# Raw memory rows and a factor behind the products in the opening of a two-layer encoder trunk

## The chip, the cores and the metric

The kernel runs on one core of one Trainium2 chip. The metric is the device time of one execution in microseconds; a kernel's time is the median of its runs. Engines are named as the profile names them: PE (TensorE, the matrix products), PEld (its weight loads), DVE (VectorE), ACT (ScalarE), POOL (GpSimd) and SP (SyncE, which here only issues transfers). L12 is line 12 of the kernel before, unless the text says otherwise.

## The reference

Two layers, each with a token mixer (dilated windows in the first, grouped queries with a rotary table in the second), cross-attention into 256 memory tokens, a gate and an output projection. D_MODEL is 1024, the sequence has 512 tokens. What matters here is the way from the memory rows to the keys and values of the first layer:

```python
def rmsnorm(x, g):
    xf = x.astype(jnp.float32)
    y = xf * lax.rsqrt(jnp.mean(xf * xf, axis=-1, keepdims=True) + EPS)
    return (y * g.astype(jnp.float32)).astype(x.dtype)
...
def memory_attention(q_mem, mem_h, w_kv, qn_g, kn_g):
    ...
    kv = jnp.einsum('bnd,de->bne', mem_h, w_kv).reshape(Bn, N, 2, MEM_HEADS, HEAD_DIM)
    k = rmsnorm(kv[:, :, 0], kn_g)
    v = kv[:, :, 1]
...
    for i in range(DEPTH):
        h = rmsnorm(x, norm_g[i])
        mem_h = rmsnorm(mem, mem_norm_g[i])
```

`mem_h` is `mem` times a factor for each row (the reciprocal root mean square) times the norm's row `mem_norm_g[i]`. The factor of a row is one number for a whole token, so it may stand in front of the product with `w_kv` or behind it. `x` is normalized in the same way by `norm_g[i]`.

## The kernel before

All arithmetic is on the chip. Products have nearly full float32 precision: each operand is split into an upper part (rounded to the product's format) and a lower part (what is left), and each product runs as three, upper by upper, lower by upper, upper by lower. In `proj_t`, `mm_early` issues the first two (L173, L174) for each of four blocks of the inner dimension, and `mm_late` then the third (L177). The large projections use a Strassen-like scheme of seven products (`s_chunk`), whose operands are sums of quarters of x and of the weights.

**Order.** Each engine works through its own instructions in the order in which the program issues them, and so do the queues of transfers; waits between engines follow from the data. The order is written by hand. A driver counts slots: after each group of products `W.advance()` and `drv.tick()` issue what is due (weight casts, norms, splits). Work that is spawned with a delay appears in the tick of that slot; what follows a finished group (`drv.release`, `drv.free`) one or two groups later.

**Weights** come as pieces of 128x1024 float32 (512 KB), issued on SP's queue by `W.dma` as long as fewer than a set number are live. `W.hi` casts a piece on ACT into the upper part `wh` (L309), `W.lo` makes the lower part `wo` on DVE (L319); both live in rings of four tiles, so the fifth cast waits for the last product with the first piece. For the Strassen chunk, `W.sum` also adds pieces on DVE (L278) or by accumulating transfers from POOL's queue.

**The opening** (L938 to L1046). SP's queue: the two norm rows as single rows of 4 KB, the two blocks of memory rows (128 tokens each) with weights between them, more weights, the four blocks of x and weights. `row_bank` (L622) spreads a norm row over 128 partitions by a product with a column of ones; this is done for both rows, two halves each, eight passes at L627. The memory rows go through `norm_1` (squares with a sum on ACT or DVE, then three small operations on POOL for the factor), `norm_2` (L497: row block times factor times norm row, on DVE), `turn4` (four transpositions on PE, L503) and `split` (L159: upper part on ACT, lower part on DVE). `ahead` is called by `chunk` ahead of a group and issues the other three half blocks: one ahead of the second group, two ahead of the third. It also copies x's norm row out of the PSUM banks (L1024).

**Keys and values.** `mem_kv` (L657) runs two projections over two blocks and two halves of the inner dimension: four groups for the keys, four for the values. The keys' evacuation `ev_k` takes head-wise squares on ACT (`head_sq`, L594), a factor on POOL (`rstd_of`, L450 and L451), multiplies on DVE (`head_mul`, L599), transposes and splits. `ev_v` writes half the values as an upper part on ACT (L676) and a lower one on DVE (L679).

**x.** `prep` (L963) starts at slot 2: `norm_1` of a block in each slot, `norm_2` one slot later, `first_t` (transpositions and splits of the top half, L161, L164) one slot after that, then differences for the Strassen scheme. `rm` keeps the memory rows' factors for the second layer.

## Time and profile before

| what | value |
|---|---|
| median of 3 runs | 956.26 us (955.84 to 957.37) |
| the profiled execution's own time | 955.53 us |
| its span in the profile | 953.7 us |
| PE busy | 942.1 us, 99% of the span |
| DVE busy | 789.9 us, 83% |
| ACT busy | 680.5 us, 71% |
| POOL busy | 332.9 us, 35% |
| moved by transfers | 202.98 MB |

In rows of the timeline the first number is the start and the second the duration, both in microseconds from the start of the span; then engine, line, operation, the tiles written and read with their shapes, how many such instructions the row merges, and in brackets how long the engine was idle before the row and what ended that. In rows of the chain of waits there are start, duration and what the time went to. In groups, the numbers behind the bar are the busy time in microseconds and the mean duration in nanoseconds, then the idle time before them. A row of transfers gives the number, the size of each and the median time in microseconds from its issue to its landing. "Issue" as a cause means that the profile shows nothing that the engine waited for.

### The profile page before, as it was taken

The numbers are of one execution on the slowest core, as the hardware profiler recorded it, in microseconds if no ns is written. First come the engines' busy times: TensorE is split into PE (matmuls) and PEld (weight loads), VectorE is DVE, ScalarE is ACT, GpSimd is POOL, SyncE is SP. The second block draws the span as 40 slices with busy tenths as digits, with TensorE's granted clock in tenths as the row PEclk, the third lists the DMA queues.
The fourth block names the chain that finished last, engine by engine and source line by source line (L and its number), as shares of the span: only waits on it lengthen the run. The fifth ranks groups of instructions, "written<-read, shape, count | busy, mean of one in ns | idle before, by whom it ended". The sixth has DMA issues, their size and how long they took to land.

```text
span 953.7 us, 16568 instructions
## 1 busy us (share of the span) xinstructions
PE 942.1 (99%) x5682; PEld 831.7 (87%) x5682; DVE 789.9 (83%) x1410; ACT 680.5 (71%) x1701; POOL 332.9 (35%) x478
## 2 busy tenths in 40 slices
PE   8999999999999999999999999999899999999998
PEld 4879888888888888888889998888899999998886
DVE  4898776878888888979788899977988898769982
ACT  5875689686868686867775667547778877879860
POOL 1512423557454546463726111213232330111110
PEclk9999999999999999999999999999999999999999
DMA  9989946969687869696877989979966697877524
GB/s 357 329 205 344 301 113 175 295 117 267 145 262 155 264 156 265 155 263 135 236 185 184 260 199 252 291 264 299 246 153 133 193 237 173 210 208 179 126 56 128
DMA packets 85913, 202.98 MB, mean 213 GB/s; under 512 B 25027, under 2 KB 34499, under 8 KB 85829
## 3 DMA queue, kind: packets, MB, share of 16 engines
q1 hardware_dynamic: 66676, 138.94, 42.7%
q0 software_dynamic: 17856, 60.83, 34.4%
q10 hardware_dynamic: 1296, 2.16, 0.6%
q8 instruction: 45, 0.74, 0.3%
q14 instruction: 40, 0.32, 0.1%
HBM read 155.96 MB, written 11.34 MB: 175 GB/s over the span
## 4 chain that ended last, share of the span: by engine, by line
PE 90%; DVE 5%; ACT 2%; DMA 1%; issue 1%; POOL 0%; DVEq 0%; SPq 0%; ACTq 0%; POOLq 0%
PE pj L174 23%; PE pj L173 23%; PE pj L177 23%; PE qT L606 2%; DVE wo L319 2%; PE sa L1162 1%; PE oo L1270 1%; PE pt L1249 1%; PE ptb L1472 1%; PE sa L1158 1%; PE ob L177 1%; PE xT L503 1%; PE row L627 1%; PE pmt L736 1%; PE ob L174 1%
## 5 line engine op out<-in xcount | busy, mean ns | idle before, releaser
L319 DVE TENSOR_TENSOR wo<-wl,wh 128x1024 fp32r<-128x1024 f32 x255 | 316.0, 1245 | 6.2 <-ACT wh L309 6.0
L309 ACT CAST wh<-wl 128x1024 fp32r<-128x1024 f32 x255 | 268.3, 1059 | 30.5 <-PE pj L174 14.4
L173 PE MATMUL pj<-wh,hS 128*128 128x512 f32 (+1 forms) x448 | 157.4, 365 | 0.8 <-DVE sn L403 0.8
L174 PE MATMUL pj<-wh,hS 128*128 128x512 f32 (+1 forms) x448 | 152.2, 353 | 0.6 <-DVE hS L570 0.6
L173 PE MATMUL pj<-wh,h 128*128 128x512 f32 (+1 forms) x336 | 117.9, 364 | 0.0
L174 PE MATMUL pj<-wh,h 128*128 128x512 f32 (+1 forms) x336 | 114.2, 353 | 1.1 <-DVE h L570 1.1
L451 POOL TENSOR_TENSOR rstd<-mse,half 128x4 f32<-128x4 f32 (+2 forms) x96 | 100.9, 1051 | 8.0
L177 PE MATMUL pj<-wo,hS 128*128 128x512 f32 (+1 forms) x448 | 100.0, 352 | 0.2 <-DVE wo L319 0.2
L173 PEld LDWEIGHTS pj<-wh,hS 128*128 128x128 f32 x448 | 84.8, 189 | 11.3 <-DVE sn L403 1.0
L174 PEld LDWEIGHTS pj<-wh,hS 128*128 128x128 f32 x448 | 84.9, 190 | 11.0 <-DVE hS L570 0.8
L450 POOL TENSOR_SCALAR mse<-hss 128x4 f32<-128x4 f32 (+1 forms) x86 | 42.5, 494 | 126.3 <-ACT junk L594 122.1
L177 PEld LDWEIGHTS pj<-wo,hS 128*128 128x128 f32 x448 | 74.6, 189 | 12.4 <-DVE wo L319 0.6
L594 ACT ACTIVATE junk<-sn 128x128 f32<-128x128 f32 x264 | 79.1, 309 | 1.0 <-DVE sn L397 1.0
L386 ACT COPY sn<-pj 128x512 f32<-128x512 f32 x116 | 64.5, 590 | 21.1 <-PE pj L177 20.3
L1106 POOL TENSOR_TENSOR ta<-sn,tabs 128x128 f32<-128x128 f32 (+1 forms) x64 | 35.5, 562 | 119.0 <-DVE sn L599 92.2
L177 PE MATMUL pj<-wo,h 128*128 128x512 f32 (+1 forms) x336 | 74.8, 352 | 0.0
L174 PEld LDWEIGHTS pj<-wh,h 128*128 128x128 f32 x336 | 63.7, 190 | 8.8 <-DVE h L570 1.3
L173 PEld LDWEIGHTS pj<-wh,h 128*128 128x128 f32 x336 | 63.6, 189 | 7.3
L403 DVE TENSOR_TENSOR sn<-pj,sn 128x512 f32<-128x512 f32 x87 | 59.3, 683 | 10.1 <-PE pj L177 7.7
L293 POOL DMA_DIRECT2D wl<-wl x33 | 29.2, 884 | 106.8 <-DVE wo L319 59.6
L177 PEld LDWEIGHTS pj<-wo,h 128*128 128x128 f32 x336 | 56.0, 189 | 8.8
L283 POOL DMA_DIRECT2D wl<-wl x33 | 31.3, 982 | 62.5 <-DVE wl L278 18.5
(246 smaller groups left out, 2358.7 us busy)
## 6 DMA issues: line engine op xcount, KB each, us to landing
wl<-in_wall_dram SPq DMA_DIRECT2D x222, 512.0 KB, 7.3
wl<-wl POOLq DMA_DIRECT2D x66, 512.0 KB, 5.6
wl<-in_wall_dram POOLq DMA_DIRECT2D x42, 512.0 KB, 8.3
od<-o SPq DMA_DIRECT2D x11, 256.0 KB, 5.6
og<-od SPq DMA_DIRECT2D x10, 256.0 KB, 7.6
m<-in_mem_dram SPq DMA_DIRECT2D x4, 512.0 KB, 5.7
x<-in_x_dram SPq DMA_DIRECT2D x4, 512.0 KB, 8.9
v0d<-sn SPq DMA_DIRECT2D x8, 256.0 KB, 7.3
```

The costliest lines, as they stand in the source:

```text
L173: T.matmul(o, a, b, start=start, stop=False, skip_group_check=True)
L174: T.matmul(o, c, d, start=False, stop=False, skip_group_check=True)
L177: T.matmul(o, a, b, start=False, stop=stop, skip_group_check=True)
L283: G.dma_start(self.tile[key], self.tile[c, "T1", x], accum_op=ALU.add)
L309: A.copy(wh, self.tile[self.items[i]])
L319: V.tensor_tensor(wo, self.tile[key], wh.bitcast(F32), ALU.subtract)
L386: A.copy(t, b)
L403: V.tensor_tensor(t, b, t, ALU.subtract if q == "12" else ALU.add)
L450: G.tensor_scalar(e, ss, EPS, None, ALU.add)
L451: G.tensor_tensor(r, e, half[:, 0:n], ALU.pow)
L594: A.activation(jk, p[:, j * 128:(j + 1) * 128], AF.Square, scale=QS, accum_out=ss[:, j:j + 1])
L1106: G.tensor_tensor(ta[:, 0:n], xn[:, 0:n, 0:32], ropeA[:, 0, b, s0:s0 + n], ALU.mult)
```

## The change

The memory rows of the first layer are no longer multiplied by their factor ahead of the transposition: they are multiplied by the norm's row alone, split and projected, and the factor of each row comes into the evacuation: as the scale of the keys' head-wise squares and a multiply on POOL of the keys' head factors (`ev_k`), and as the scale of the values (`ev_v`). `rm` grows from two columns to six: the factor, the factor by QS, half the factor.

The norm's row of the memory comes in two ways: its first half is spread by one product with the column of ones (two passes), its second half and the whole row for x come as transfers that write all 128 partitions. The memory rows are loaded as four half blocks. The first half of the norm's row is issued on ACT's queue, the rest on SP's in a new order. The products of x's row, its copies and the `busy` product are gone. Four products on a tile of zeros (`idle`) are issued: two ahead of the spread row, one behind it, one behind the first transposition.

The transpositions and splits of the three later half blocks are issued in the middle of a group, between the early and the late products (`mid` instead of `pre`): one in the first group, two in the second, so each a group earlier than before. The first half block's upper part is written by DVE instead of ACT. All squares of the memory rows are on ACT. The casts of the third and fourth weight piece are issued in the first group.

```diff
 TCKW = {}
 NBIG, NM4, NS2, SCRATCH = 7, 23, 14, 2048
 RING, LEAD = 4, 2
-BULK, ACTIVE, SET_AT, WARM, MEM_B, PREP_Y, PREP_B, HALF, SET_B = 2, 2, 15, 1, 14, 1, 1, {"a": 3, "b": 3, "o": 0}, 9
+BULK, ACTIVE, SET_AT, IDLE, MEM_B, PREP_Y, PREP_B, HALF, SET_B = 2, 2, 15, (2, 1, 1), 14, 1, 1, {"a": 3, "b": 3, "o": 0}, 9
 MEM_STEP = 1, 1
 MEM_D = 4
 DIRECT, DIRECT_B = (7,), (4, 5, 6, 7)
...
 
     W = Weights()
 
-    def chunk(units, nb, group, evac, pre=None):
+    def chunk(units, nb, group, evac):
 
         ps = [None] * nb
         for u in range(units):
...
             for b in range(nb):
                 if u == 0:
                     ps[b] = pj()
-                if pre:
-                    pre(u, b)
                 group(w, u, b, ps[b])
                 drv.free()
                 if u == units - 1:
...
     mask = tabs[:, 0:512]
     ropeA = tabs[:, 512:2048].rearrange("p (c b s e) -> p c b s e", c=2, b=4, s=6)
     half = pool.tile([128, 8], F32, name="half")
-    rm = pool.tile([128, 2], F32, name="rm")
+    rm = pool.tile([128, 6], F32, name="rm")
     ones = tabs[0:1, 0:128]
     V.memset(half, -0.5)
     V.memset(ones, 1.0)
...
 
     NAT = [nat(b) for b in range(4)]
 
-    def proj_t(act, sels, evac, pre=None):
+    def proj_t(act, sels, evac, mid=None):
 
         def group(w, u, b, p):
             for k in range(4):
                 kk = 4 * u + k
                 mm_early(p, sels[b](act, 0, kk), w[k][0], sels[b](act, 1, kk), w[k][0], kk == 0)
+            if mid:
+                mid(u, b)
             for k in range(4):
                 kk = 4 * u + k
                 mm_late(p, sels[b](act, 0, kk), w[k][1], kk == 7)
-        chunk(2, len(sels), group, evac, pre)
+        chunk(2, len(sels), group, evac)
 
     part = {}
 
...
         put("22", f22)
         yield 1
 
-    def head_sq(p, n=4):
+    def head_sq(p, n=4, by=QS):
         ss = sm(n, "hss")
         for j in range(n):
             jk = small.tile([128, 128], F32, tag="junk", name="junk", bufs=2)
-            A.activation(jk, p[:, j * 128:(j + 1) * 128], AF.Square, scale=QS, accum_out=ss[:, j:j + 1])
+            A.activation(jk, p[:, j * 128:(j + 1) * 128], AF.Square, scale=by, accum_out=ss[:, j:j + 1])
         return rstd_of(ss, n)
 
     def head_mul(p, r, n=4, dst=None):
...
         t = m4(name="row")
         nc.sync.dma_start(t, src.to_broadcast([128, D]))
         rows[name] = halves(t)
-
-    def row_bank(name, times=1, bank=at):
-
-        r = [bank("row") for _ in range(2)]
-        for j in (1, 0):
-            for _ in range(times):
-                T.matmul(r[j], ones, rows[name][j][0:1, :], start=True, stop=True)
-        return r
 
     Ms = {}
 
...
         drv.soon(lambda: V.scalar_tensor_tensor(lo, q, gain, hi.bitcast(F32), ALU.mult, ALU.subtract))
         yield 1
 
-    def mem_kv(layer, M, pre=None):
+    def mem_kv(layer, M, mid=None):
         kt_ = [m4(F32R, "kmT").rearrange("p (h t) -> p h t", h=4) for _ in range(2)]
         vt_ = [m4(F32R, "vm").rearrange("p (b e) -> p b e", b=2) for _ in range(2)]
 
         def ev_k(b, p):
-            r = head_sq(p)
+            r = head_sq(p) if layer else head_sq(p, by=rm[:, 2 + b:3 + b])
 
             def rest():
+                if not layer:
+                    G.tensor_scalar(r, r, rm[:, b:b + 1], None, ALU.mult)
                 xn = head_mul(p, r)
                 yield 2
                 q = transpose4(xn)
...
 
         def ev_v(b, p):
 
-            A.activation(vt_[0][:, b], p, AF.Copy, scale=0.5)
+            h = 0.5 if layer else rm[:, 4 + b:5 + b]
+            A.activation(vt_[0][:, b], p, AF.Copy, scale=h)
             if b and LO_V[layer]:
                 yield LO_V[layer]
-            V.scalar_tensor_tensor(vt_[1][:, b], p, 0.5, vt_[0][:, b].bitcast(F32), ALU.mult, ALU.subtract)
-            yield 1
-
-        proj_t(M, NAT[:2], ev_k, pre)
+            V.scalar_tensor_tensor(vt_[1][:, b], p, h, vt_[0][:, b].bitcast(F32), ALU.mult, ALU.subtract)
+            yield 1
+
+        proj_t(M, NAT[:2], ev_k, mid)
         proj_t(M, NAT[:2], ev_v)
         return kt_, vt_
 
...
     xt = [m4(name="x") for _ in range(4)]
     rows = {}
     mt = [m4(name="m") for _ in range(2)]
+    row0 = m4(name="row0")[0:1, 0:512]
+    nc.scalar.dma_start(row0, mem_norm_g[0:1, 0:512])
     nc.scalar.dma_start(ident, ident_d)
-    row0 = m4(name="row0")[0:1, :]
-    nc.sync.dma_start(row0, mem_norm_g[0:1, :])
-    rows["m0"] = halves(row0)
-    row1 = m4(name="row1")[0:1, :]
-    nc.sync.dma_start(row1, norm_g[0:1, :])
-    rows["x0"] = halves(row1)
+    row1 = s2(name="row1")
+    nc.sync.dma_start(mt[0][:, 0:512], mem[0:128, 0:512])
+    W.dma(2)
+    nc.sync.dma_start(mt[1][:, 0:512], mem[128:256, 0:512])
+    nc.sync.dma_start(row1, mem_norm_g[0:1, 512:1024].to_broadcast([128, 512]))
     for b in range(2):
-        nc.sync.dma_start(mt[b], mem[b * 128:(b + 1) * 128])
-        W.dma(1)
+        nc.sync.dma_start(mt[b][:, 512:1024], mem[b * 128:(b + 1) * 128, 512:1024])
+    W.dma(2)
+    row_load("x", norm_g[0:1, :])
     W.dma(2)
     tabA = s2(name="tabA")[:, 0:256].rearrange("p (b c d) -> p b c d", b=2, c=4)
     grA = s2(name="grA")[:, 0:192].rearrange("p (s c) -> p s c", s=6)
     nc.sync.dma_start(gc, gcol)
     for c in range(4):
         nc.sync.dma_start(xt[c], xv[c])
-        if c % 2:
+        if c % 2 and c < 3:
             W.dma(2)
     H, H2 = {}, {}
     xb = [halves(t) for t in xt]
...
                             grA[:, None].to_broadcast([128, 4, 6, 32]), ALU.mult)
             yield 1
 
-    first = row_bank("m0", WARM)
-    gain = row_bank("x0", 1, pj)
-    rows["x"] = halves(m4(name="row"))
-
-    def busy(n):
-
-        T.matmul(at("busy")[:, 0:n], ones, rows["m0"][0][0:1, 0:n], start=True, stop=True)
-
+    z = s2(F32R, "z")
+    V.memset(z.bitcast(F32), 0.0)
+
+    def idle(n):
+
+        for _ in range(n):
+            T.matmul(at("idle"), z[:, 0:128], z, start=True, stop=True)
+
+    idle(IDLE[0])
+    row = at("row")
+    T.matmul(row, ones, row0, start=True, stop=True)
     mb, M = [halves(t) for t in mt], Act(NM)
-    nst = [norm_1(mb[0], True)]
+    ss = [sm(2, "ss") for _ in range(2)]
+    mg = {}
+
+    def times(b, j):
+
+        t = mg[b, j] = s2(name="mg")
+        V.tensor_tensor(t, mb[b][j], row1 if j else row, ALU.mult)
+
+    def square(b, j):
+
+        A.activation(s2(name="sq"), mb[b][j], AF.Square, scale=1.0 / 32.0, accum_out=ss[b][:, j:j + 1])
+
+    def factor(b):
+
+        e = sm(1, "mse")
+        G.tensor_tensor(e, ss[b][:, 0:1], ss[b][:, 1:2], ALU.add)
+        r = rstd_of(e, 1)
+        for k, by in enumerate((1.0, QS, 0.5)):
+            G.tensor_scalar(rm[:, 2 * k + b:2 * k + b + 1], r, by, None, ALU.mult)
+
+    def place_m(b, j, act=True, p=None):
+
+        cs = slice(b * 128, (b + 1) * 128)
+        split(M.block(0, j, cs), M.block(1, j, cs), p or turn4(mg[b, j], None, None), act)
+
+    square(0, 0)
+    times(0, 0)
+    idle(IDLE[1])
+    p = turn4(mg[0, 0], None, None)
+    idle(IDLE[2])
     W.hi(True)
-    norm_2(mb[0], nst[0], first, (0,))
-
-    def mid():
-        busy(128)
-        W.lo()
-        nst.append(norm_1(mb[1]))
-
-    turn4(mb[0][0], M.block(0, 0, slice(0, 128)), M.block(1, 0, slice(0, 128)), mid)
+    place_m(0, 0, False, p)
     W.hi(True)
-    norm_2(mb[1], nst[1], first, (0,))
     W.lo()
+    times(1, 0)
+    W.lo()
+    for b, j in ((1, 0), (0, 1), (1, 1)):
+        square(b, j)
+    for b in range(2):
+        times(b, 1)
+        factor(b)
 
     def ahead(u, b):
 
+        if (u, b) == (0, 0):
+            place_m(1, 0)
+            W.hi(True)
+            W.hi(True)
         if (u, b) == (0, 1):
-            for j in range(2):
-                A.copy(rows["x"][j], gain[j])
-            norm_3(mb[1], M, 128, 0)
-            for c in range(2):
-                G.tensor_copy(rm[:, c:c + 1], nst[c])
-            for c in range(2):
-                norm_2(mb[c], nst[c], first, (1,))
-        if (u, b) == (1, 0):
-            for c in range(2):
-                norm_3(mb[c], M, 128 * c, 1)
+            place_m(0, 1)
+            place_m(1, 1)
 
     drv.spawn(prep(), PD)
     drv.spawn(setup(), SET_AT)
```

## The prediction

> **What bounds the kernel now.** I read the page first, then the stretches, the opening in order of time, and last the chain of waits.
>
> ```profile
> span 953.7 us, 16568 instructions
> PE 942.1 (99%) x5682; PEld 831.7 (87%) x5682; DVE 789.9 (83%) x1410; ACT 680.5 (71%) x1701; POOL 332.9 (35%) x478
> ```
>
> TensorE lacks 953.7 - 942.1 = 11.6 us of the whole span. A microsecond that the opening gives or takes therefore has almost nowhere to be absorbed once TensorE alone sets the pace. Between 30 and 60 us it does not: VectorE is as full as TensorE there.
>
> ```profile
> 30.00:40.00 10.00, 10.00 (x56) 8.54 (x55) 9.81 (x13) 7.59 (x22) 6.48 (x10) 1.00 0.93 331
> 40.00:50.00 10.00, 10.00 (x52) 8.32 (x51) 9.53 (x13) 6.13 (x10) 2.37 (x4) 1.00 0.99 243
> 50.00:60.00 10.00, 9.79 (x43) 7.54 (x42) 9.84 (x15) 8.34 (x13) 2.01 (x3) 1.00 0.92 170
> 59.38 1.19 PE L177 MATMUL pj<-wo,hS 128*128 128x512 f32 x4 [0.21 <-DVE wo L319]
> ```
>
> The columns are the stretch, PE, PEld, VectorE, ScalarE and POOL busy, granted clock, transfer share and GB/s. VectorE is busy 9.81, 9.53 and 9.84 of 10, the transfers are at 0.92 to 0.99, and the one wait of TensorE, at 59.38, is for VectorE. So the opening has two clocks that both must move: TensorE, and VectorE's unbroken queue from 30 us on. Now the first 12 us:
>
> ```profile
> 1.40 0.36 SPq L950 DMA_DIRECT2D m<-in_mem_dram  x1
> 2.35 7.16 PE L627 MATMUL row<-row,tabs 1*128 1x512 f32 x8 [2.35 <-DMA row<-in_mem_norm_g_dram]
> 5.26 0.63 ACT L490 ACTIVATE sq<-m 128x512 f32<-128x512 f32 x1 [3.04 <-DMA m<-in_mem_dram]
> 6.66 1.04 ACT L309 CAST wh<-wl 128x1024 fp32r<-128x1024 f32 x1 [0.68 <-DMA wl<-in_wall_dram]
> 7.32 0.75 DVE L497 SCALAR_TENSOR_TENSOR m<-m,rstd,row 128x512 f32<-128x512 f32 x1 [1.36 <-POOL rstd L451]
> 9.45 1.12 PE L503 MATMUL xT<-ident,m 128*128 128x128 f32 x4
> 10.60 0.58 ACT L161 CAST act<-xT 128x512 fp32r<-128x512 f32 x1 [1.30 <-PE xT L503]
> 11.22 0.69 DVE L164 TENSOR_TENSOR act<-xT,act 128x512 fp32r<-128x512 f32 x1 [2.01 <-ACT act L161]
> 11.24 0.79 PE L173 MATMUL pj<-wh,act 128*128 128x512 f32 x1
> 13.61 0.43 PE pj L173
> 15.20 0.93 PE pj L177 x4
> 18.47 0.23 PE pj L173
> ```
>
> The normalized memory half is ready at 7.32 + 0.75 = 8.1 us, but TensorE is inside the eight row passes until 9.5 us; only then come the transpositions, the split, and the first product at 11.24. The last three rows are steps of the chain: a product costs 0.43 until about 15.2 (the group of four there takes 0.93, 0.23 each) and 0.23 after. What follows the first group:
>
> ```profile
> 9.37 0.19 POOL L492 TENSOR_TENSOR mse<-ss 128x1 f32<-128x1 f32 x1 [2.08 <-ACT sq L490]
> 17.97 0.50 PE L174 MATMUL pj<-wh,act 128*128 128x512 f32 x1 [0.22 <-DVE act L164]
> 18.98 0.63 ACT L490 ACTIVATE sq<-x 128x512 f32<-128x512 f32 x1
> 19.15 2.35 DVE L319 TENSOR_TENSOR wo<-wl,wh 128x1024 fp32r<-128x1024 f32 x2
> 20.40 1.15 POOL L492 TENSOR_TENSOR mse<-ss 128x1 f32<-128x1 f32 x1 [9.60 <-ACT sq L490]
> 23.06 1.40 DVE L497 SCALAR_TENSOR_TENSOR x<-x,rstd,row 128x512 f32<-128x512 f32 x2
> 28.34 0.65 ACT L490 ACTIVATE sq<-x 128x512 f32<-128x512 f32 x1
> 29.57 1.08 ACT L161 CAST h<-xT 128x512 fp32r<-128x512 f32 x2
> 30.19 1.29 DVE L164 TENSOR_TENSOR h<-xT,h 128x512 fp32r<-128x512 f32 x2 [1.00 <-ACT h L161]
> 30.66 0.57 POOL L451 TENSOR_TENSOR rstd<-mse,half 128x1 f32<-128x1 f32 x1
> 31.40 0.68 DVE L599 TENSOR_TENSOR xn<-pj,rstd 128x512 f32<-128x512 f32 x1
> 34.26 1.22 DVE L278 TENSOR_TENSOR wl<-wl 128x1024 f32<-128x1024 f32 x1
> 37.26 0.57 POOL L451 TENSOR_TENSOR rstd<-mse,half 128x1 f32<-128x1 f32 x1
> 37.92 0.68 DVE L599 TENSOR_TENSOR xn<-pj,rstd 128x512 f32<-128x512 f32 x1
> ```
>
> VectorE's last idle microsecond ends at 30.19, and what ends it is ScalarE's split of x's first block (29.57), itself queued behind the squares at 28.34. That is where the shift must be measured.
>
> **First product.** Six of the eight row passes go; so do the squares, POOL's factor and the multiply by it ahead of the first transposition. The new path: a zero fill on VectorE (no row for one of 128x512; between nothing and the 0.69 of L164, taken near the top, since the half it fills is as long), two fill products at 0.43, and the row pair at 7.16 / 4 = 1.8. From 1.0 that is 1.0 + 0.7 + 0.9 + 1.8 = 4.4 us, or 3.7 with a free fill. The first half block, now first on its queue and half as large, lands near 0.73 + 3.86 - 0.65 = 3.9 (0.73 is where the first issue stands now; 3.86 is the landing at 5.26 less the issue at 1.40; 0.65 is half of 1.3 per 512 KB, from the 1.4 between the landings that ended the waits before 5.26 and 6.66 and the 1.25 of the rows under transfers below). Multiply 0.7, transposition 1.1, split on VectorE instead of ScalarE 0.6 to 0.7: first product at 6.9, against 11.24, **4.3 earlier**. The first weight lands near 5.2 and its cast of 1.04 ends at 6.3, in time. The third fill product ends before the multiply does, the fourth before the split: nothing, covered by these; each would cost 0.43 without the cover.
>
> **Second group.** Seven more products at 0.43 after the lower half (7.6) end at 10.6. The next rows' transposition (0.5 to 1.1), cast 0.58 and split 0.69 put the group's second product at 12.6 to 13.0, against 17.97: 5 earlier. VectorE alone comes to the same: from 6.2 it has the two passes of the first split, three multiplies and the next split, 6 x 0.69, and two weight residues at 2.35 / 2, 6.5 together, so 12.7. It holds this point there even if TensorE were faster. The group then ends at 13 + 7 x 0.23 + 8 transpositions (0.9) + 0.93 = 16.2.
>
> **ScalarE from there.** One group of the page is needed:
>
> ```profile
> L594 ACT ACTIVATE junk<-sn 128x128 f32<-128x128 f32 x264 | 79.1, 309 | 1.0 <-DVE sn L397 1.0
> ```
>
> With four weight tiles split early, the casts of the fifth and sixth move one group ahead. They wait for the ring slots that this group's end frees (a new wait; queued behind it are the squares of x's first two blocks): 16.2 + 2 x 1.0 = 18.2. Squares of x0 and x1, 1.25 each (the 29.57 - 28.34 of x2's): 20.7; four head squares, 79.1 / 264 = 0.3 each: 21.9; two casts: 23.9; squares of x2: 25.2. Then comes the split that started at 29.57: **4.4 earlier**. x0's normalization comes 23.06 - 18.98 = 4.1 after its squares start, so at 22.3 to 23.7, and its transposition ends at 24.6, in time; TensorE waits some 1.5 us ahead of it and is then about 4.4 earlier too.
>
> **Transfers.** The new rows are 256 KB and 512 KB spread over all partitions.
>
> ```profile
> 599.75 0.43 SPq L260 DMA_DIRECT2D wl<-in_wall_dram  x1
> 601.10 0.33 SPq L619 DMA_DIRECT2D row<-in_mem_norm_g_dram  x1
> wl<-in_wall_dram SPq DMA_DIRECT2D x1, 512.0 KB, 7.2
> row<-in_mem_norm_g_dram SPq DMA_DIRECT2D x1, 512.0 KB, 7.1
> ```
>
> A spread row of this size landed 601.10 + 7.1 = 608.2, 1.25 after the weight ahead of it (599.75 + 7.2): it costs what any 512 KB cost, 1.3. So the queue grows by 1.5 x 1.3 = 1.9 us. By the new order ten such pieces (six weights, one and a half of memory rows, one and a half of the new rows, and x0 itself) land after the first half block, so x0 near 3.9 + 13 = 16.9, x1 18.2, and x2 after two more weights 22.1; squares want them at 18.2, 19.5 and 23.9. The fifth and sixth weights, just ahead of x0, land at 14.3 and 15.6 and are wanted at 16.2. Margin 1.3 at the least, so nothing. The next narrow place is the sum at 34.26, wanted at 30 to 31 now:
>
> ```profile
> 18.33 0.33 SPq L260 DMA_DIRECT2D wl<-in_wall_dram  x1
> wl<-in_wall_dram SPq DMA_DIRECT2D x1, 512.0 KB, 10.2
> ```
>
> The piece it needs landed at 28.5 and will at 30.4: just in time, 0 to 0.5.
>
> **The factor behind the products.** Keys get a second POOL multiply of 128x4 ahead of VectorE's `head_mul`, queued behind the next x block's norm.
>
> ```profile
> L450 POOL TENSOR_SCALAR mse<-hss 128x4 f32<-128x4 f32 x2 | 2.0, 1001 | 2.1 <-ACT junk L594 2.0
> ```
>
> That norm ended at 30.66 + 0.57 = 31.2 and at 37.8, against heads at 31.40 and 37.92. With 1.0 (the row above; the operation itself has no row) the heads wait until 32.2 and 38.8, 0.8 and 0.9. The second is mostly covered: after the first, VectorE is 0.8 late and POOL, which waits for ScalarE, is not. I take **0.9** for both; ends 0.3 and 1.8. POOL's six extra factor operations of the opening end near 13, wanted at 20.8: nothing. Scales that become columns: taken at 0.1, between nothing and 0.2.
>
> The Trainium skill (SBUF — State Buffer, Who interferes with whom) says that a VectorE instruction with two SBUF inputs and a GpSimd instruction that reads SBUF exclude each other for a whole instruction. The rows agree: the same 128x1 add took 0.19 at 9.37 and 1.15 at 20.40 beside the residue. By this rule POOL runs freely once VectorE stands waiting for it, which would make the stall 0.3 to 0.5 rather than 0.9.
>
> **Sum.** 4.4 - 0.9 - 0.1 - 0.1 (half of what the sum may wait, rounded down) = 3.3 us at 30 us, on VectorE; TensorE has more, so at 59.38 VectorE decides, and 3.3 travels to the end. The profiled execution took 955.53, so 952.2; the median of the runs, 956.26, lies 0.73 above it. **Predicted: 956.26 - 3.3 = 953.0.** Its own range: with a late clock (1.3, third rival), a stall of 1.8, 0.5 at the sum and 0.2 for the scales 0.6 of the 4.4 is left, but not all of them are likely at once; I take a gain of 1.9 to 4.7, so 951.6 to 954.4.
>
> The Trainium skill (TensorE: Matmul & The Clock Gate, Part 1) has the clock double after about 3.4 us of sustained activity. Here TensorE was inside row passes from 2.35 to 9.5 and the step stayed 0.43 until 15.2, 3.9 after the first full product: one-row passes did not count as activity. If the zero products count, the rate is up before the first group; since VectorE holds the second group to about 12.7, that is worth 0.4 at most.
>
> **Rivals.**
> - *Transfers bind the stretch to 60 us (slower).* For: share 0.92 to 0.99, and everything from the sum at 34.26 on needs pieces queued behind the new rows. If that piece and its followers set VectorE's pace, the start is worth nothing and 786 KB are added: 1.9 us at the opening's pace, 3.2 at the 243 GB/s of 40 to 50 us, so 958.2 to 959.5 on the median. It decides once the piece of 28.5 lands 5.8 late or the pieces behind it have no slack. Against: that 5.8 of slack (34.26 - 28.5), and that in the view of waits of the first 60 us no engine but ScalarE at 6.66 and the first memory rows waits for a transfer. 0.16.
> - *POOL binds.* Each added multiply costs VectorE its full turn twice, up to 1.9 each: 4.4 - 3.8 - 0.1 = 0.5, 955.8. For: POOL's norm ends 0.1 to 0.2 before the heads. Against: VectorE's first wait covers the second. 0.16.
> - *The slow rate lasts a window longer.* If it takes 7.8 instead of 3.9 after the first product, some nine products and four transpositions cost 0.2 or 0.15 more, of which 0.6 is hidden by VectorE: 1.3 to 1.9 lost, 954.6. For: gaps between the first products are more than before. 0.12.
> - *No stall at all and full rate early:* 4.4 + 0.4 or more, below 951.6. 0.08.
>
> **Chances.** Forecast 0.48. Faster by over 0.2% (1.9 us, about what a measurement can tell from none): forecast, last rival and half of the third, 0.62. Within: the second and the rest of the third, 0.22. Slower: 0.16. The range reaches from half of the last rival, 950.9, to the lower edge of the first, 958.2, leaving about 0.18 out.
>
> **What would show it.** First product near 6.9; `row` two passes; second product of group two near 12.8. The split of x's first block near 25.2 and VectorE unbroken from 25.8, with one idle below 1 us ahead of the first `xn` ended by POOL. Squares of x not ended by a transfer. A wait of the sum at L278 for a transfer, or TensorE at 0.43 after 12 us, would make it wrong; so would a first product after 8.5.

## The result, and the profile after

The changed kernel is slower, where the prediction had it 3.3 us faster.

| | before | after |
|---|---|---|
| median | 956.82 us (955.84 to 957.47, 4 runs) | 964.25 us (963.02 to 964.47, 4 runs) |
| ratio to before, 95% interval | | 1.0076 (1.0058 to 1.0093) |
| the profiled execution: time, span | 955.53, 953.7 us | 964.47, 962.7 us |

The busy times from the page of after:

```profile
PE 940.2 (98%) x5678; PEld 831.8 (86%) x5678; DVE 790.1 (82%) x1410; ACT 682.0 (71%) x1700; POOL 339.6 (35%) x484
```

TensorE's work has shrunk (940.2 against 942.1 us) and the span has grown by 9.0. What was added is idle time of TensorE: 22.5 us against 11.6. The stretches of 10 us of after show where; the columns are those of the table of before in the prediction:

```profile
10.00:20.00 10.00, 9.77 (x46) 7.62 (x45) 9.07 (x12) 7.71 (x14) 6.71 (x12) 1.00 1.03 411
20.00:30.00 10.00, 3.08 (x14) 2.22 (x12) 0.61 (x1) 6.13 (x20) 4.55 (x12) 0.76 1.02 409
30.00:40.00 10.00, 5.96 (x21) 5.03 (x22) 8.56 (x11) 4.08 (x13) 0.24 (x1) 0.56 0.68 268
```

Until 20 us the opening is fuller than before (TensorE 9.77 here, 9.10 in the same stretch of before). Then VectorE works 0.61 us in 10, and TensorE 3.08. The timeline of after at this place names the cause in the row of L278:

```profile
19.40 1.22 DVE L319 TENSOR_TENSOR wo<-wl,wh 128x1024 fp32r<-128x1024 f32 x1
20.19 0.39 PE L173 MATMUL pj<-wh,act 128*128 128x512 f32 x1
21.06 0.57 POOL L449 TENSOR_TENSOR rstd<-mse,half 128x1 f32<-128x1 f32 x1
31.44 1.23 DVE L278 TENSOR_TENSOR wl<-wl 128x1024 f32<-128x1024 f32 x1 [10.82 <-DMA wl<-in_wall_dram]
32.58 1.41 DVE L495 SCALAR_TENSOR_TENSOR x<-x,rstd,row 128x512 f32<-128x512 f32 x2
34.05 1.97 PE L501 MATMUL xT<-ident,x 128*128 128x128 f32 x8 [10.97 <-DVE x L495]
```

VectorE's first sum for the Strassen chunk (L278) waits 10.82 us for its piece of the weights. x's first norm (L495) is queued behind it. Its factor had been ready since 21.63 (21.06 + 0.57), so without the sum it could have started some ten microseconds earlier. Before, by the prediction's rows, the norm of x's first block starts at 23.06 and the first sum at 34.26, behind the norms of two blocks of x, a split, a head multiply and four residues. After, the sum stands ahead of all of them. TensorE, whose next work in its queue is the transposition of x, idles for 10.97.

The chain of waits of after, cut to 0 to 40 us, goes through the same point and shows the price on TensorE's side:

```profile
23.81 8.77 DMA wl<-in_wall_dram
34.05 1.97 PE xT L501 x8
36.01 0.43 PE pj L173
38.95 0.24 PE pj L174
```

The last three rows: after the gap eight transpositions take 1.97, and the products step at 0.43 again until 38.95, with a granted clock of 0.56 in the stretch from 30 to 40. So the gap costs more than its length. As a mark by which kernels can be compared I use the products that read `hS`, of the first Strassen chunk; these rows of the view of that tile (from 40 to 110 us; durations, then first and last start) are of before and of after:

```profile
L177 PE MATMUL pj<-wo,hS x64: 283/336/497, 56.3 to 99.3; 128*128 128x512 f32 x32, 128*128 128x256 f32 x32
```

```profile
L177 PE MATMUL pj<-wo,hS x64: 282/336/389, 64.5 to 107.0; 128*128 128x512 f32 x32, 128*128 128x256 f32 x32
```

The last of them comes 7.7 us later, which agrees with the medians (964.25 - 956.82 = 7.4): what the change does to the time is done by then. The account: the fourth group, the last before the gap, starts 5.0 earlier (20.19 against 25.23); the gap adds 10.97; the eight products behind it take 39.19 - 36.01 = 3.2 instead of eight times 0.23, 1.3 more; the transpositions 1.97 instead of the 0.87 that eight take in the chain of before, 1.1 more. That is 8.3, and 0.6 of it is caught up by the mark. The rows of before that it uses, from the chain and the timeline:

```profile
28.12 0.87 PE xT L503 x8
```

```profile
25.23 0.39 PE L173 MATMUL pj<-wh,act 128*128 128x512 f32 x1
```

The opening itself did get shorter. Its rows of after:

```profile
1.61 1.22 PE L1000 MATMUL idle<-z 128*128 128x512 f32 x2 [1.61 <-DVE z L995]
3.10 2.07 PE L1004 MATMUL row<-row,tabs 1*128 1x512 f32 x2 [0.27 <-DMA row<-in_mem_norm_g_dram]
5.21 0.69 DVE L1012 TENSOR_TENSOR mg<-m,row 128x512 f32<-128x512 f32 x1 [3.65 <-PE row L1004]
6.37 1.09 PE L501 MATMUL xT<-ident,mg 128*128 128x128 f32 x4 [0.48 <-DMA ident<-in_ident_dram]
8.34 0.77 PE L173 MATMUL pj<-wh,act 128*128 128x512 f32 x1 [0.45 <-ACT wh L309]
11.60 0.39 PE L174 MATMUL pj<-wh,act 128*128 128x512 f32 x1
12.18 1.17 PE L177 MATMUL pj<-wo,act 128*128 128x512 f32 x4
13.83 0.50 PE L174 MATMUL pj<-wh,act 128*128 128x512 f32 x1 [0.23 <-DVE act L164]
27.35 0.33 POOL L658 TENSOR_SCALAR rstd<-rstd,rm 128x4 f32<-128x4 f32 x1
```

First product at 8.34 instead of 11.24, the second group's second at 13.83 instead of 17.97. ScalarE is through with the squares of x's third block at 25.40 + 0.64 = 26.0, where before its split started at 29.57, but there is nothing to split.

**Why the sum moved.** The code gives the link, since no engine's row shows it. `advance` calls `sum` in each group, and a sum of kind T1 is due LEAD = 2 groups after the load of its piece was issued, whether or not it has landed. Loads are issued while the number of live pieces is below a limit, and `lo` takes a piece off that number once its lower part is made. The change casts the third and fourth piece in the first group, so their lower parts are issued in the advance of that group too: four pieces are off instead of two, the loads that the sums need are issued two groups earlier in the program, and the two sums stand two groups earlier in VectorE's queue (behind groups 2 and 3, counted from 0, instead of 4 and 5). The transfers do not land earlier for it, since their queue is full (1.02 and 1.03 in the stretches above).

### The profile page after: what moved, and what is told of

The parts are those of the page before. It is cut to its first block, busy times and chain, and to the rows that moved or that the text cites. A ratio compares the mean times of both kernels' runs of the same rounds, so it can differ in the third digit from the quotient of the medians.

```text
span 962.7 us, 16569 instructions
## 1 busy us (share of the span) xinstructions
PE 940.2 (98%) x5678; PEld 831.8 (86%) x5678; DVE 790.1 (82%) x1410; ACT 682.0 (71%) x1700; POOL 339.6 (35%) x484
## 4 chain that ended last, share of the span: by engine, by line
PE 89%; DVE 4%; ACT 3%; DMA 3%; issue 1%; POOL 0%; SPq 0%; DVEq 0%; ACTq 0%; POOLq 0%
PE pj L174 24%; PE pj L173 24%; PE pj L177 23%; PE qT L606 2%; PE oo L1294 1%; DMA wl<-in_wall_dram 1%; PE pt L1273 1%; PE sa L1186 1%; PE ptb L1496 1%; PE sa L1182 1%; DVE wo L319 1%; PE xT L501 1%; DMA odb<-o 1%; PE ob L177 1%; PE pmt L731 1%
## 5 line engine op out<-in xcount | busy, mean ns | idle before, releaser
L1130 POOL TENSOR_TENSOR ta<-sn,tabs 128x128 f32<-128x128 f32 (+1 forms) x64 | 37.5, 595 | 117.9 <-DVE sn L599 91.1
L293 POOL DMA_DIRECT2D wl<-wl x33 | 29.3, 887 | 111.5 <-DVE wo L319 76.3
L594 ACT ACTIVATION_READ_ACCUMULATOR junk<-sn 128x1 f32 x264 | 52.2, 198 | 0.0
```

What stands on the lines that cost most here:

```text
L293: G.dma_start(self.tile[key], self.tile[c, "T2", x], accum_op=ALU.add)
L594: A.activation(jk, p[:, j * 128:(j + 1) * 128], AF.Square, scale=by, accum_out=ss[:, j:j + 1])
L1130: G.tensor_tensor(ta[:, 0:n], xn[:, 0:n, 0:32], ropeA[:, 0, b, s0:s0 + n], ALU.mult)
```

## The experiments

All ratios are to runs of the kernel before on the same chip.

**The order alone, put into the kernel before (before_live).** One line of `dma` lets two more pieces be live in the advance of group 0. The loads keep their order, and nothing else of the change is in this kernel.

```diff
-            while self.allocs and self.live < KEEP[self.allocs[0][2]] and most:
+            while self.allocs and self.live < KEEP[self.allocs[0][2]] + 2 * (self.g == 0) and most:
```

> The kernel before with one number changed: in the first advance (group 0) the limit of live weight pieces is two higher, so that six pieces are issued there instead of four and the two sums at L278 stand two groups earlier in VectorE's order, the first of them ahead of x's norm; nothing of the opening is changed. Theory (the order of the sum alone makes the gap): VectorE waits at the sum from about 23 to the piece's landing near 28.5, x's first transposition comes near 31 instead of 28, TensorE has a gap of about 3 us, 958.5 to 961 us, ratio 1.0025 to 1.005. Rival (the gap comes from the new transfers or the new opening): no change, ratio 1.000.

960.47 us against 955.5, ratio 1.0048 (1.0034 to 1.0062). The timeline of this kernel:

```profile
30.24 1.23 DVE L278 TENSOR_TENSOR wl<-wl 128x1024 f32<-128x1024 f32 x1 [6.75 <-DMA wl<-in_wall_dram]
32.90 1.94 PE L503 MATMUL xT<-ident,x 128*128 128x128 f32 x8 [4.44 <-issue]
```

The same sum, ahead of x's norm again, waits 6.75 for its piece (which lands near 30.2 here, not at the 28.5 that I had expected), and TensorE idles for 4.44 (the row's "issue" hides that it is x's norm that is late). The kernel before has the gap without new rows, raw memory rows or a factor behind the products: the place in the queue alone makes it.

**The change, with the sum held back (hold4, hold5).** The sums of the first chunk are not issued ahead of group 4, or group 5:

```diff
                         continue
+                    if c == 0 and self.g < 5:
+                        continue
                     V.tensor_tensor(self.tile[key], self.tile[key], self.tile[c, "11", x], ALU.add)
```

> The changed kernel with one line more: the two sums of the Strassen chunk's first weights on VectorE (L278) may not be issued before group 4, where they stood before the change. Theory (the sum moved two groups ahead in VectorE's queue, in front of x's norm, and waits there for a piece that lands at 31.4 us): the 11 us gap of TensorE is gone, the first x transposition comes near 23 to 24 us, VectorE reaches the sum near 30 and waits at most 1.5 us for the piece; 952.5 to 954.5 us, ratio to before 0.9955 to 0.9975. Rival (transfers bind the stretch, the wait only moves): VectorE or ScalarE waits for transfers elsewhere for some 5 us or more, 956 to 962, ratio 0.999 or above.

> As the one before, but not before group 5. Theory: the piece has landed when VectorE gets there, no wait for a transfer is left, 951.5 to 953.5 us, ratio 0.9945 to 0.9965, 0.5 to 1.5 us below the one held to group 4. Rival (transfers bind): no better than the one held to group 4, 956 or above.

954.32 us, 0.9985 (0.9976 to 0.9993), with group 4; 954.12, 0.9986 (0.9977 to 0.9995), with group 5. The loss is gone, and a gain is there that is smaller than I had expected; the 0.5 to 1.5 us that I had expected between the two kernels are not there either. With group 4 the sum still waits, and with group 5 it does not (no wait stands in its row); rows of the two:

```profile
33.11 1.23 DVE L280 TENSOR_TENSOR wl<-wl 128x1024 f32<-128x1024 f32 x1 [1.94 <-DMA wl<-in_wall_dram]
```

```profile
35.52 0.69 DVE L601 TENSOR_TENSOR xn<-pj,rstd 128x512 f32<-128x512 f32 x1 [0.51 <-POOL rstd L660]
36.12 1.21 DVE L280 TENSOR_TENSOR wl<-wl 128x1024 f32<-128x1024 f32 x1
```

In the execution traced of hold4 the piece lands at 33.1, and whatever wants it earlier waits. In that of hold5 it was issued at 20.85 and landed 10.2 later, at 31.1, well before VectorE comes to the sum. The loads up to this piece stand in the same order in both kernels, so its landing differs by 2 us between two executions.

**The change without the two early casts (casts_late).** `ahead` no longer calls `W.hi(True)` twice in the first group, which takes the cause away where the change put it in.

> The changed kernel without the two early weight casts in the first group (the third and fourth piece are then cast where they were before). Nothing else is edited: the live count of pieces then falls a group later, the loads and with them the sums go back to where they stood. Theory: most of the gap goes by this alone; the third group starts about 1 us later than in the changed kernel, 953 to 955 us, ratio 0.996 to 0.998. Rival (transfers bind): 957 or above. Rival (the early casts are what makes the opening fast): the third group starts 3 us later, 956.

955.17 us, 0.9996 (0.9987 to 1.0005): no gap, and no gain that can be told. In its timeline the first sum is back behind the norms, the split and the head multiply, and starts near where it did before (34.26):

```profile
7.36 1.09 PE L501 MATMUL xT<-ident,mg 128*128 128x128 f32 x4 [1.65 <-DMA ident<-in_ident_dram]
19.19 0.50 PE L173 MATMUL pj<-wh,act 128*128 128x512 f32 x1 [0.74 <-ACT wh L309]
29.68 1.29 DVE L164 TENSOR_TENSOR h<-xT,h 128x512 fp32r<-128x512 f32 x2 [1.00 <-ACT h L161]
33.93 1.22 DVE L278 TENSOR_TENSOR wl<-wl 128x1024 f32<-128x1024 f32 x1
```

The third group waits 0.74 for a cast, and of the lead of the opening 0.5 is left at the split of x's first block (29.68, before 30.19). Not all of this loss is the casts': in this execution the first transposition also waits 1.65 for the identity matrix, where it waits 0.48 in after. The nearer comparison is hold5, where it waits 1.29 and the first product stands at 9.08, against 9.32 here. There the same split comes 1.4 earlier:

```profile
28.32 1.29 DVE L164 TENSOR_TENSOR h<-xT,h 128x512 fp32r<-128x512 f32 x2 [1.67 <-ACT h L161]
```

Of this, 0.24 is the first product's; so the early casts are worth about 1.1 us at this point. The medians of the two kernels are 1.05 apart, with intervals that overlap. The early casts are what keeps most of the lead, and what brings the sum forward.

**The transfers alone (before_rows, extra_load).** The two rows that the change loads in place of products (256 and 512 KB) are added to the kernel before, behind the memory rows; nothing reads them.

> The kernel before with the two new row transfers (256 KB and 512 KB spread over the partitions) added in front of its third weight; nothing reads them. Theory: landings from there on come 1.9 us later, the sum at L278 had 5.8 us of slack, x had 4 or more: ratio 1.000 to 1.0005. Rival (transfers bind the stretch to 60 us): 1.9 us or more slower, ratio 1.002 or above.

955.76 us, 0.9999 (0.9990 to 1.0008). The 786 KB by themselves cost nothing in the kernel before: the rival by which the transfers bind is out there. In the changed kernel it is another matter, by one more 512 KB that nothing reads behind x's row:

> The changed kernel with one more transfer of 512 KB (memory rows into a tile that nothing reads) behind x's norm row. Theory (TensorE's gap ends when the sum's piece lands): the sum starts 1.3 us later, near 32.7 instead of 31.44, and the end moves by as much, 965.2 to 966, ratio to before 0.001 to 0.002 above that of the changed kernel. Rival (the gap is set by ScalarE, POOL or the clock): no change.

965.46 us, 1.0101 (1.0087 to 1.0115) against 1.0076 for the change, and the sum later still:

```profile
7.76 1.09 PE L501 MATMUL xT<-ident,mg 128*128 128x128 f32 x4 [2.20 <-DMA ident<-in_ident_dram]
33.97 1.23 DVE L278 TENSOR_TENSOR wl<-wl 128x1024 f32<-128x1024 f32 x1 [11.32 <-DMA wl<-in_wall_dram]
```

It moved by 2.5, not by the 1.3 that the piece should cost; the identity was 2.2 late in this execution, so the opening's own transfers had lost time too, and I can't divide the 2.5 between the two; the landing of the same piece differs by 2 us between hold4 and hold5 without a byte added. That the gap ends with the queue of transfers is shown; its rate by this run is not.

**What is left of the predicted gain.** With the sum out of the way the gain is 1.6 to 1.8 us (955.90 less the two medians), not 3.3. In the kernel held to group 5 the first transposition waits for the identity, second on ACT's queue behind the half row:

```profile
7.12 0.66 PE L503 MATMUL xT<-ident,mg 128*128 128x128 f32 x2 [1.29 <-DMA ident<-in_ident_dram]
```

So the two change places (hold5_ident); in a second kernel (hold5_ident_noidle) the four products of zeros are left out as well (IDLE = 0, 0, 0):

```diff
-    nc.scalar.dma_start(row0, mem_norm_g[0:1, 0:512])
     nc.scalar.dma_start(ident, ident_d)
+    nc.scalar.dma_start(row0, mem_norm_g[0:1, 0:512])
```

> The kernel held to group 5, with the identity matrix ahead of the norm's half row on ScalarE's queue, as it was before the change. In the held kernel the first transposition waited 1.3 us for the identity. Theory: that wait goes, the first product comes near 7.9 instead of 9.08, and at least half of it reaches the end: 952.8 to 953.6 us, ratio 0.997 to 0.998. Rival (VectorE's queue from 30 us on decides, whatever the start): 954, ratio 0.9985 as before.

> As the one before, without the four products on zeros. Theory (they bring the full rate earlier): steps of 0.43 last 0.5 to 1.5 us longer after the first product, which comes as early, 0.3 to 1 us slower than with them. Rival (they do nothing for the rate): the same time within 0.2 us.

953.7 us, 0.9978 (0.9969 to 0.9987), with the exchange; 954.42, 0.9985 (0.9976 to 0.9993), without the zero products as well. The first product did not move to where I expected it, since now the half row was late by as much. Rows of the first of the two, then of the second:

```profile
4.04 2.07 PE L1006 MATMUL row<-row,tabs 1*128 1x512 f32 x2 [1.22 <-DMA row<-in_mem_norm_g_dram]
8.88 0.76 PE L173 MATMUL pj<-wh,act 128*128 128x512 f32 x1 [0.45 <-DVE act L163]
12.24 0.63 PE L174 MATMUL pj<-wh,act 128*128 128x512 f32 x1
27.03 1.08 ACT L161 CAST h<-xT 128x512 fp32r<-128x512 f32 x2
```

```profile
9.03 0.77 PE L173 MATMUL pj<-wh,act 128*128 128x512 f32 x1 [0.87 <-ACT wh L311]
12.25 0.39 PE L174 MATMUL pj<-wh,act 128*128 128x512 f32 x1
```

A product of 0.63 in the timeline is one at the 0.43 step, one of 0.39 at 0.23. The full rate comes 3.2 after the first product without the zeros (12.25 - 9.03) and more than 3.4 after it with them. They do not bring it earlier in these two traces. The kernel without them is 0.7 us slower in the medians, as I had expected of products that bring the rate earlier, but the intervals of the two times overlap, so whether they are worth anything stays open.

In both orders something waits for what is second on ACT's queue. So the half row (2 KB) goes first on SP's queue and the identity alone on ACT's (hold5_sprow); in a second kernel (hold5_sprow_vec) the keys' multiply by the factor also goes from POOL to VectorE:

```diff
-    nc.scalar.dma_start(row0, mem_norm_g[0:1, 0:512])
+    nc.sync.dma_start(row0, mem_norm_g[0:1, 0:512])
     nc.scalar.dma_start(ident, ident_d)
```

> With the sum of the Strassen chunk held back, the kernel with the identity first on ACT's queue still had its first product at 8.88, not at the 6.9 of the prediction, because the half row, now second on that queue, landed 1.2 late. Here the half row (2 KB) goes first on SP's queue, ahead of the memory rows, and the identity alone on ACT's. Theory (what is left of the gain is lost ahead of the first product, and the rest of the opening follows it one to one): row pair from about 2.85 (behind the two fills), multiply at about 5.0, transposition at about 5.8, first product 7.5 to 8.0, ScalarE's split of x's first block near 26.0 instead of 27.0, the last product with hS of the first chunk near 96.7 instead of 97.6, time 0.9965 to 0.9975 of before. Rival (the later chain, transfers and ScalarE's queue, holds x's split wherever the first product stands): first product near 7.7, but the split still at 26.8 or later, the last hS product at 97.4 or later, ratio 0.9975 to 0.9985.

> As hold5_sprow, with the keys' multiply by the memory rows' factor on VectorE instead of POOL. Theory (POOL's queue holds the second head multiply back by 0.51, as in the two kernels before): the wait of VectorE ahead of the second xn falls from 0.51 to 0.2 or less, VectorE pays two small operations of about 0.1 to 0.2 each, the last hS product comes 0 to 0.3 earlier than in hold5_sprow, ratio within 0.0005 of it. Rival (the wait is covered further on, by a wait of TensorE for VectorE's kmT or ScalarE's sn): no difference at the last hS product, or 0.1 to 0.3 later for the two operations.

953.86 us, 0.9978 (0.9969 to 0.9987), and 953.96 us, 0.9975 (0.9966 to 0.9985). The first product is at 7.60 in both, 1.28 earlier, and the time does not follow: here the rival held. The timeline of ScalarE in the first of the two shows what it waits for ahead of x's split:

```profile
16.32 1.08 ACT L161 CAST act<-xT 128x512 fp32r<-128x512 f32 x2 [0.25 <-PE xT L503]
17.57 1.05 ACT L311 CAST wh<-wl 128x1024 fp32r<-128x1024 f32 x1 [0.17 <-DMA wl<-in_wall_dram]
18.91 1.05 ACT L311 CAST wh<-wl 128x1024 fp32r<-128x1024 f32 x1 [0.28 <-DMA wl<-in_wall_dram]
20.22 0.64 ACT L490 ACTIVATE sq<-x 128x512 f32<-128x512 f32 x1 [0.26 <-DMA x<-in_x_dram]
27.23 1.07 ACT L161 CAST h<-xT 128x512 fp32r<-128x512 f32 x2
```

Three waits in a row for transfers, 1.3 apart: ScalarE runs at the pace of the queue. The waits are 0.7 together, and the split is at 27.23, no earlier than the 27.03 of the kernel with the exchange. The transfers themselves are late in this execution: x's first block, issued at 11.10, lands 9.1 later, at 20.2. In hold5_ident it lands at 18.5 (9.90 and 8.6), and ScalarE's squares of x wait for nothing; in hold5_ident_noidle, which has the same order of transfers, it lands at 20.0 (10.92 and 9.1). So these traces do not tell whether the half row's new place made the transfers late or the execution did. The multiply moved to VectorE takes away the wait of 0.51 ahead of the second head multiply and puts two small operations into VectorE's queue. The times of the two kernels are alike: where this multiply stands makes no difference that can be told.

**Fewer bytes ahead of x (hold5_sprow_rowx).** x's row of 512 KB is wanted only by x's norm, but stands ahead of the fifth and sixth piece and of x. It goes behind x's second block:

```diff
-    row_load("x", norm_g[0:1, :])
     W.dma(2)
...
     for c in range(4):
         nc.sync.dma_start(xt[c], xv[c])
+        if c == 1:
+            row_load("x", norm_g[0:1, :])
         if c % 2 and c < 3:
```

> In hold5_sprow the first product came 1.28 earlier than in hold5_ident (7.60 against 8.88), but ScalarE's split of x's first block did not (27.23 against 27.03): its casts of the fifth and sixth piece and its squares of x's first block now each wait for a transfer (17.57, 18.91, 20.22). Theory (the transfers are the second limit of the opening, and x's row of 512 KB ahead of those pieces costs its 1.3): with x's row issued behind x's first two blocks, the pieces and the blocks land about 1.3 earlier, these three waits go, the split of x's first block starts at 26.2 to 26.6, the last product with hS comes 0.5 to 0.9 earlier than 97.9, ratio 0.9965 to 0.9972. Rival (the waits only show what ScalarE would have spent on other work, and the split is held by something else, such as VectorE's queue or the row itself, now landing later than the norm of x wants it): split at 27.0 or later, no change of the ratio beyond 0.0005.

953.12 us, 0.9970 (0.9961 to 0.9979): 2.9 us faster than before, and the fastest kernel here. Rows of its timeline, and its mark:

```profile
7.60 0.77 PE L173 MATMUL pj<-wh,act 128*128 128x512 f32 x1 [0.45 <-DVE act L163]
12.10 1.62 PE L177 MATMUL pj<-wo,act 128*128 128x512 f32 x4
16.20 1.07 ACT L161 CAST act<-xT 128x512 fp32r<-128x512 f32 x2 [1.03 <-PE xT L503]
17.16 2.01 ACT L311 CAST wh<-wl 128x1024 fp32r<-128x1024 f32 x2
26.02 1.08 ACT L161 CAST h<-xT 128x512 fp32r<-128x512 f32 x2
```

```profile
L177 PE MATMUL pj<-wo,hS x64: 282/336/498, 53.5 to 96.6; 128*128 128x512 f32 x32, 128*128 128x256 f32 x32
```

The three waits are gone, the split stands at 26.02 (expected 26.2 to 26.6), and the last product with `hS` comes 2.7 earlier than before and 1.3 earlier than in hold5_sprow (97.9; expected 0.5 to 0.9). Of the 1.2 by which the split is earlier than in hold5_sprow, 0.1 was there ahead of the waits (16.20 against 16.32 for the upper part of the memory rows). The waits are 0.7, and each of the three also parts two operations of ScalarE that overlap by 0.1 here (16.20 + 1.07 = 17.27, against the start at 17.16). But the transfers gained more than the row that was moved: x's first block lands at 18.0 (issued at 9.31, 8.7 to its landing), 2.2 earlier than in hold5_sprow, where 512 KB cost 1.3 by the prediction's rows. By the times the step is 0.0008 of before, with intervals that overlap: two single traces show it, the times do not contradict it, and how much of it is the row's place stays open.

The first product of 7.60 is not all gain either. The group of four at 12.10 takes 1.62, where after has 1.17 for the same at 12.18: TensorE is still partly at the slow rate, over 4.5 after its first product. The 0.74 by which its first product is ahead of that of after has gone by then. How long the slow rate lasts differs between executions: in hold5_sprow_vec, whose TensorE rows are the same up to 10.54, the four transpositions at 11.32 take 0.60, the fast rate, 3.7 after the first product.

## Why the prediction was wrong

**The step that failed** is in the part on transfers: "The next narrow place is the sum at 34.26, wanted at 30 to 31 now", and "just in time, 0 to 0.5". The landing in it was nearly right: 30.4 predicted, and the sum starts as it lands, at 31.44. The term stood at 0.1 in the sum (half of 0 to 0.5, which is rather 0.25); it measured 10.82. The other side was wrong: the sum was wanted from 20.6 on, where the operation ahead of it ends (19.40 + 1.22). I had moved the sum forward by the gain and kept its place among VectorE's instructions. The change moved that place by two groups. I had listed what the early casts do to ScalarE's queue and to the ring slots, but not that `lo` of the same pieces follows in the same advance and frees two loads, and that sums count from the issue of a load. The rest of the stall follows from one queue in order: behind the sum stood x's norm, behind x's norm TensorE's transposition. The run with the order alone (1.0048) and the runs with the sum held back (0.9985, 0.9986) show it from both sides.

Of the rivals none had this. The one on the slow side named the same instruction, priced it by the bytes added (1.9 to 3.2) and had it decide once the piece is 5.8 late; the piece was 2.9 later than its 28.5 and did harm for another reason. As it was put, it fell: the bytes alone change nothing (0.9999). The sign that would show the prediction wrong, a wait of the sum at L278 for a transfer, was the one that came.

**The other steps**, by the trace of after and the repaired kernels:

- *First product* at 6.9: 8.34. The zero fill took 0.48, not 0.7, but the fills 1.22, not 0.9, and the row pair 2.07, not 1.8, behind a wait of 0.27; the multiply starts at 5.21, not at 4.4. The identity, which I had not costed, adds 0.48, and latencies between engines the rest. The second group, 12.6 to 13.0, was at 13.83.
- *ScalarE's split of x's first block* at 25.2: ScalarE is free for it at 26.0 in after, and it starts at 26.02 in hold5_sprow_rowx. The lead at this point, 29.57 - 26.02 = 3.6, was put at 4.4. It was lost early: the casts of the fifth and sixth piece, put at 16.2, start at 17.16 in both, and from there ScalarE's queue took as long as the sum said. The 16.2 was itself added up wrongly (13 + 1.6 + 0.9 + 0.93 is 16.4); the third group starts at 17.36, so the second ended about a microsecond later than that.
- *Transfers hidden, margin 1.3*: in after no cast of the fifth and sixth piece and no square of x waits for a transfer, as predicted. There was no margin in hold5_sprow, where the casts of the fifth and sixth piece and the squares of x wait, 0.7 in all; in hold5_sprow_rowx, with 512 KB less ahead of them, they do not. By the landings above (18.0 to 20.2 for x's first block, put at 16.9) the scatter between executions is larger than the margin.
- *POOL's multiply*: sized at 1.0, measured 0.33. In hold5 the wait is 0.51, below the 0.9 taken, and it is at the second head multiply; the prediction put 0.8 at the first, which does not wait there, and had the second mostly covered. In after, behind the gap, the second waits 1.63. The Trainium skill's rule (SBUF — State Buffer, Who interferes with whom), which would have made the stall 0.3 to 0.5, was nearer than the row I used.
- *Scales as columns* at 0.1, between nothing and 0.2: a head square with a column takes 0.36 in after, where the same squares of before take 0.28 (the 0.309 of the prediction is the mean of all 264). From the first of the four to the cast behind them it is 1.37 (21.52 to 22.89) against 1.02 (25.43 to 26.45), so 0.35 more on ScalarE's path to the split. One of the four of after, and the first of before:

```profile
21.87 0.36 ACT L594 ACTIVATE junk<-pj,rm 128x128 f32<-128x128 f32 x1
```

```profile
25.43 0.28 ACT L594 ACTIVATE junk<-pj 128x128 f32<-128x128 f32 x1
```

- *The slow rate a window longer*: not in after, where the full rate is there at 11.60, 3.3 after the first product, against 3.9 before; but it came in part in hold5_sprow_rowx, over 4.5 after it, and in hold5, where the group of four at 13.57 takes 2.00: four steps of 0.43, so the slow rate lasts to about 15.3, 6.2 after the first product at 9.08. The rate was no cause of the miss, and it can take away part of what an earlier first product brings.
- *The lead travels to the end*: most of it does. In hold5_sprow_rowx it is 3.6 at ScalarE's split of x, 2.7 at the mark near 97 and 2.9 in the medians.

That the repaired kernel's 953.12 lies at the predicted 953.0 says little: it has x's row and the half row elsewhere, and the sum held by hand.

## What to carry to other kernels

When a change moves work earlier in a program whose order comes from counters (live buffers, groups since a load was issued), write out the new order of each engine's queue before any durations are summed; a time from the old trace belongs to an instruction at its old place. An operation on a queue in order that waits for a transfer should stand behind everything that is ready before the transfer lands, and be due by landing, not by issue. When one limit of an opening is taken away, look which transfer is wanted next: here 1.3 us at the first product brought nothing that the times could tell, while ScalarE waited three times for pieces and x. And since the same load landed up to 2 us earlier or later from one execution to the next, a margin of 1.3 that is read from one trace is not safe.

## What the runs showed of the hardware

- After an idle stretch of 11 us TensorE's step is 0.43 again, for 4.9 us from the first transposition (34.05 to 38.95). After the 4.44 idle in the kernel before with the order alone it is so as well (0.63 is the 0.43 step; at 36.27 a product takes 0.39 again):

```profile
35.49 0.63 PE L173 MATMUL pj<-wh,act 128*128 128x512 f32 x1
```

  The Trainium skill (TensorE: Matmul & The Clock Gate, Part 1) says that the clock is halved after an idle window of about 3.4 us; both gaps agree. The profile's granted clock shows it there (0.56 in the stretch from 30 to 40 of after), but stands at 1.00 in the stretch from 10 to 20, where TensorE is slow until 11.6 as well.
- A small transfer, second on ACT's queue, landed at very different times in executions of the same opening: the first transposition waited 0.48 for the identity in after, 1.29 in hold5, 1.65 in casts_late and 2.20 in extra_load, and not at all in hold4; these openings are the same as far as that transposition. The 2 KB of the half row made the product wait at most 0.27 as the first transfer of ACT's queue, 1.22 as its second (hold5_ident), and not at all as the first of SP's.
- Large loads scatter too. x's first block, behind the same transfers in the same order, landed at 18.3 in hold5 (issued at 9.85, 8.4 to its landing) and at 20.2 in casts_late (10.33 and 9.9).
